# Moving the stationary weight blocks of a decoder trunk 224 bytes aside in SBUF

## The chip, the cores and the metric

The kernel runs on one core of a Trainium2 chip. The metric is the device time of one execution in microseconds. The kernel before takes 851.81 us, the median of three runs (850.81 to 852.27 us).

## The reference, cut to what matters

A two-layer decoder trunk over 256 tokens with 1024 features, all in float32. Layer 0 mixes tokens with a gated unit (gMLP), layer 1 with an mLSTM; behind each stand a LayerNorm with residual, a SwiGLU feed-forward, a second LayerNorm and a gated embedding.

```
for i in range(DEPTH):                       # DEPTH = 2
    y = gmlp_mixer(x, ...) if i % 2 == 0 else mlstm_mixer(x, ...)
    x = layer_norm(ALPHA * x + y, ln1_g[i], ln1_b[i])
    x = layer_norm(ALPHA * x + (silu(x @ w_gate) * (x @ w_up)) @ w_down, ln2_g[i], ln2_b[i])
    x = x + sigmoid(x @ ple_w_gate[i] + ple_b_gate[i]) * (p[i] @ ple_w_proj[i])
```

Nearly all of the arithmetic is the products with the weights: `gm_w_in`, `gm_w_out`, `ml_w_in`, `ml_w_out`, `ffn_w_gate`, `ffn_w_up`, `ffn_w_down` and `ple_w_gate`.

## The kernel before, in words

Every product is done with float32 numbers split in two float32r parts, hi and lo: `a @ b` becomes hi·hi + lo·hi + hi·lo, three matmuls into one PSUM bank. The weights come from HBM in blocks of 128 partitions by 1024 float32 (512 KB). For each block SyncE loads a `raw` tile, ScalarE casts it to the hi half of a tile `w`, and VectorE subtracts to get the lo half (`split`, L134 to L136). `weight_plan` writes down the order of all blocks; `weight` (L175) hands out the next one and keeps loads eight blocks and casts four blocks ahead of their use. A `w` tile has 2 × 1024 float32, 8192 bytes in each partition, and the pool keeps six such slots; blocks that are used for longer lie in the wider pool `b8`.

There are two ways in which a block meets x or a hidden state.

- As the moving operand (`mm_tok`, L206 to L209, and `mm_part`): 128 tokens of the other operand are the stationary 128 columns, and 512 columns of the weight stream past them. So run the gMLP's v columns (`vps`), all down projections (`acc`), the first 512 columns of gate, up and z (`first`, `zf`), and the embedding's gate (`gate`).
- As the stationary operand (`mm_feat`, L211 to L214, called by `feat_from_x`, L216): 128 columns of the weight are loaded, and x^T, 256 tokens in `xh` (hi) or `xl` (lo), streams past. A block gives 8 × 3 = 24 such matmuls. So run the gMLP's u columns (`ups`, 24 blocks), the mLSTM's xm columns (`xmps`, 16), the later z columns (`zps`, 12), and the later gate and up columns of both layers (`pg` and `pu`, 36 each).

Each MATMUL on TensorE has its own LDWEIGHTS, which loads the stationary 128 columns of that matmul while the matmul before it still streams; the profile shows these loads as an engine of their own, PEld.

In SBUF the program lays every large tile at a multiple of 512 bytes. `xh` and `xl` hold 8 pieces of 1024 bytes, a `w` tile 2 × 8 pieces of 512 bytes. So a stationary piece of `w` and the x^T piece that streams meanwhile both start at a multiple of 512.

The order of work is written out by hand in the loops; no scheduler changes it. TensorE's order around the change is, for a step of the gMLP: 24 matmuls of `ups`, 4 of `svps`, 12 of `acc`; for a step of the feed-forward: 24 of `pg`, 24 of `pu`, 12 of `acc`; for a step of the mLSTM: 24 of `xmps`, then a dozen small ones for q, v, the gates and the scores, and at some steps 24 of `zps`. The gates' matmuls (`psG`, L691 and L700) are a case of their own: x^T's place is taken by `xm`, 256 columns as well, and the stationary operand `wx` has only 16 columns.

Of the kernel before, what the change touches and what calls it, by code (L numbers as in the profile page):

```python
# [9 lines left out]
F32R = mybir.dt.float32r  # L10
# [4 lines left out]
P = 128  # L15
D = 1024
# [30 lines left out]
WIDE = {(n, l, k) for l in range(2) for n, m in (("g", 4), ("u", 2), ("pg", 6)) for k in range(m)}  # L47
# [5 lines left out]
def down_blocks(f):  # L53

    return range(4) if f == 3 + LAG else [f - LAG] if f > 3 + LAG else []


def weight_plan(a):
# [17 lines left out]
    def ffn(l):  # L76
        add(("pj", l, 0), a["ple_proj"][l, 0])
        for n in ("g", "u"):
            for kp in range(4):
                add((n, l, kp), a["ffn_" + n][l, kp])  # L80
        for f in range(4, NF + LAG):
            for n in ("g", "u") if f < NF else ():
                add((n, l, f), a["ffn_" + n][l, f])
            for e in down_blocks(f):
                add(("d", l, e), a["ffn_d"][l, e])
        add(("pj", l, 1), a["ple_proj"][l, 1])
        for k in range(KD):
            add(("pg", l, k), a["ple_gate"][l, k])
# [28 lines left out]
def trunk(ctx, tc, a, out):  # L117
# [10 lines left out]
    def tl(tag, shape, dt=F32, name="t"):  # L128
        return sb.tile(shape, dt, tag=tag, name=name, bufs=BUFS[tag])
# [4 lines left out]
    def split(hi, lo, src, fast=False, sub=dve):  # L134

        return dve.tensor_copy(hi, src) if fast else act.copy(hi, src), sub.tensor_tensor(lo, src, hi.bitcast(F32), ALU.subtract)  # L136
# [7 lines left out]
    def issue_after(ops):  # L144

        stack = ExitStack()
        for op in ops:
            stack.enter_context(tc.issue_after(op.ins))
        return stack
# [3 lines left out]
    def ahead(loads, casts):  # L153
        while at["load"] < min(len(plan), at["use"] + loads):
            ap = plan[at["load"]][1]
            n = ap.shape[-1]
            t = tl("raw", [P, n], name="raw")
            for c in HALF if at["load"] == 0 else [slice(0, n)]:
                sp.dma_start(t[:, c], ap[:, c])
            raws[at["load"]] = t  # L160
            at["load"] += 1
        while at["cast"] < min(len(plan), at["use"] + casts):
            i = at["cast"]
            key, raw = plan[i][0], raws.pop(i)
            n = raw.shape[-1]
            t = tl("b8" if key in WIDE else "w", [P, 2, D], F32R, "w")
            with issue_after(behind["cast"]):
                for c in HALF if i == 0 else [slice(0, n)]:
                    split(t[:, 0, c], t[:, 1, c], raw[:, c], fast=i == 0 and c.start == 0)
            wt[i] = t  # L170
            at["cast"] += 1
# [3 lines left out]
    def weight(*key, casts=None):  # L175
        at["use"] = max(at["use"], place[key])
        ahead(LOAD_AHEAD, CAST_AHEAD if casts is None else casts)
        at["use"] = max(at["use"], place[key] + 1)
        return wt.pop(place[key])
# [126 lines left out]
    for i in range(4):  # L306
        t = tl("m2", [P, 2, S], name="xr")
        if i == 0:
            for k in range(2):
                act.dma_start(t[:, k, :], a["xT"][i, :, k, :])  # L310
        else:
            sp.dma_start(t, a["xT"][i])
        ahead(1 + i, int(i == 0))
        xr.append(t)
    make_identity(nc, ident)
    pool.memset(mhalf, -0.5)
    for i in range(4):
        for k in ((0,), (1,)) if i == 0 else ((0, 1),):
            c, cr = slice(2 * i + k[0], 2 * i + k[-1] + 1), slice(k[0], k[-1] + 1)
            split(xh[:, c, :], xl[:, c, :], xr[i][:, cr, :], fast=c.start == 0)  # L320
            ahead(LOAD_AHEAD, 1 + i)

    vs = []
    for c in range(6):
# [21 lines left out]
        for kp in range(4):  # L346
            w = weight("v", c, kp)
# [90 lines left out]
    def channel_mixer(l, acc, last, hook=None):  # L438
# [60 lines left out]
        for f in range(4, NF + LAG):  # L499
            if f < NF:  # L500
                gate_up(f)
            if f == 4:
                transpose_h(1)
                acc = Down(NF)
            for e in down_blocks(f):
                acc.add(e, hs.pop(e), weight("d", l, e, casts=1 if f >= NF else None))
            if f == 14 and hook:
                hook()
            if f == NF - 1:
                ahead(LOAD_AHEAD, LAG + 1)  # L510
# [449 lines left out]
```

## Time and profile before

| | |
|---|---|
| median of three runs | 851.81 us |
| the profiled execution, its own time | 852.55 us |
| its span, first to last instruction | 850.8 us |
| TensorE busy (matmuls) | 842.0 us, 99% of the span |
| weight loads on TensorE busy | 761.8 us, 90% |
| VectorE, ScalarE, GpSimd busy | 580.2, 452.9, 154.9 us |
| DMA queue of the loads | 54.3% of 16 engines' time |
| mean granted TensorE clock | 0.999 |

A matmul's time in the profile runs from its start to a modelled end behind the array's drain, and the next one starts before that end. So how fast matmuls follow each other is read from start to start, not from the duration of one.

### The profile page before, as it was taken

To read this page: it belongs to the slowest core of one execution; us is meant where nothing else is said; L and a number is where in the kernel's file an instruction comes from. 1 tells how busy PE (TensorE), PEld (TensorE's weight loads), DVE (VectorE), ACT (ScalarE), POOL (GpSimd) and SP (SyncE) were. 2 spreads that over 40 slices of the span, in tenths; PEclk is the share of its full clock that TensorE was granted. 3 is DMA by queue.
4 is the path that set the end of the run, shared out by engine and by line. 5 is a ranking of instruction groups with operands and counts; after the bars stand their busy time and mean duration, and the time that the engine had idled before them with its cause. 6 is when DMAs were issued, how large, how long until landed. Compare 5 with 4: busy or idle time off the path is not lost.

```text
span 850.8 us, 13770 instructions
## 1 busy us (share of the span) xinstructions
PE 842.0 (99%) x5367; PEld 761.8 (90%) x5367; DVE 580.2 (68%) x831; ACT 452.9 (53%) x722; POOL 154.9 (18%) x197
## 2 busy tenths in 40 slices
PE   8999999999999999999999999999999999999997
PEld 6889999998889999999879999998888999999986
DVE  6667985676955555465868877688895555466574
ACT  6556655455444444365247767777643444455422
POOL 1021653443100001500102333233310000000010
PEclk9999999999999999999999999999999999999999
DMA  8885465567375555577234444263745655577601
GB/s 296 294 290 175 149 201 176 173 204 262 119 266 183 194 179 189 177 256 261 70 122 148 153 127 136 74 235 108 240 161 197 207 178 195 176 244 251 197 2 50
DMA packets 44714, 155.62 MB, mean 183 GB/s; under 512 B 5224, under 2 KB 5992, under 8 KB 44648
## 3 DMA queue, kind: packets, MB, share of 16 engines
q1 hardware_dynamic: 44360, 154.47, 54.3%
q8 instruction: 42, 0.69, 0.3%
q10 hardware_dynamic: 288, 0.26, 0.1%
q14 instruction: 24, 0.20, 0.1%
HBM read 153.67 MB, written 1.05 MB: 182 GB/s over the span
## 4 chain that ended last, share of the span: by engine, by line
PE 95%; DVE 2%; DMA 1%; POOL 0%; ACT 0%; issue 0%; DVEq 0%; SPq 0%; ACTq 0%
PE acc L207 9%; PE acc L208 9%; PE acc L209 9%; PE pu L214 4%; PE pu L213 4%; PE pu L212 4%; PE pg L214 4%; PE pg L213 4%; PE pg L212 4%; PE ups L214 3%; PE ups L213 3%; PE vps L207 3%; PE ups L212 3%; PE vps L208 3%; PE vps L209 3%; PE xmps L212 2%
## 5 line engine op out<-in xcount | busy, mean ns | idle before, releaser
L136 DVE TENSOR_TENSOR w<-raw,w 128x1024 fp32r<-128x1024 f32 (+1 forms) x277 | 334.5, 1219 | 168.0 <-ACT w L136 167.2
L136 ACT CAST w<-raw 128x1024 fp32r<-128x1024 f32 (+1 forms) x276 | 284.7, 1040 | 200.2 <-issue 54.5
L207 PE MATMUL acc<-w,h 128*128 128x512 f32 x336 | 131.8, 392 | 0.9 <-ACT hn L833 0.9
L208 PE MATMUL acc<-w,h 128*128 128x512 f32 x336 | 131.5, 391 | 0.2 <-DVE h L136 0.2
L209 PE MATMUL acc<-w,h 128*128 128x512 f32 x336 | 130.7, 389 | 0.0
L212 PE MATMUL pg<-xh,w 128*128 128x256 f32 x288 | 81.6, 283 | 0.0
L214 PE MATMUL pu<-xh,w 128*128 128x256 f32 x288 | 81.5, 283 | 0.0
L212 PE MATMUL pu<-xh,w 128*128 128x256 f32 x288 | 81.5, 283 | 0.0
L213 PE MATMUL pu<-xl,w 128*128 128x256 f32 x288 | 81.5, 283 | 0.0
L214 PE MATMUL pg<-xh,w 128*128 128x256 f32 x288 | 81.5, 283 | 0.0
L213 PE MATMUL pg<-xl,w 128*128 128x256 f32 x288 | 81.5, 283 | 0.0
L209 PEld LDWEIGHTS acc<-w,h 128*128 128x128 f32 x336 | 63.1, 188 | 13.5
L207 PEld LDWEIGHTS acc<-w,h 128*128 128x128 f32 x336 | 63.3, 188 | 13.0 <-ACT hn L833 1.3
L208 PEld LDWEIGHTS acc<-w,h 128*128 128x128 f32 x336 | 63.3, 188 | 11.5 <-DVE h L136 0.6
L212 PEld LDWEIGHTS pg<-xh,w 128*128 128x128 f32 x288 | 55.1, 191 | 1.3
L213 PEld LDWEIGHTS pg<-xl,w 128*128 128x128 f32 x288 | 55.1, 191 | 1.3
L265 POOL TENSOR_SCALAR ve<-mv 128x1 f32<-128x1 f32 x8 | 6.2, 776 | 273.8 <-DVE mv L285 273.8
L212 PEld LDWEIGHTS pu<-xh,w 128*128 128x128 f32 x288 | 55.3, 192 | 0.0
L213 PEld LDWEIGHTS pu<-xl,w 128*128 128x128 f32 x288 | 55.3, 192 | 0.0
L214 PEld LDWEIGHTS pu<-xh,w 128*128 128x128 f32 x288 | 55.3, 192 | 0.0
L214 PEld LDWEIGHTS pg<-xh,w 128*128 128x128 f32 x288 | 55.1, 191 | 0.0
L214 PE MATMUL ups<-xh,w 128*128 128x256 f32 x192 | 54.3, 283 | 0.0
(237 smaller groups left out, 1806.9 us busy)
## 6 DMA issues: line engine op xcount, KB each, us to landing
raw<-in_ffn_g SPq DMA_DIRECT2D x44, 512.0 KB, 3.5
raw<-in_ffn_u SPq DMA_DIRECT2D x44, 512.0 KB, 3.5
raw<-in_ffn_d SPq DMA_DIRECT2D x44, 512.0 KB, 3.6
raw<-in_gm_u SPq DMA_DIRECT2D x24, 512.0 KB, 3.5
raw<-in_gm_wo SPq DMA_DIRECT2D x24, 512.0 KB, 3.5
raw<-in_gm_v SPq DMA_DIRECT2D x23, 512.0 KB, 4.9
raw<-in_ple_gate SPq DMA_DIRECT2D x16, 512.0 KB, 4.4
raw<-in_ml_z SPq DMA_DIRECT2D x16, 512.0 KB, 3.5
```

The costliest lines, as they stand in the source:

```text
L136: return dve.tensor_copy(hi, src) if fast else act.copy(hi, src), sub.tensor_tensor(lo, src, hi.bitcast(F32), ALU.subtract)
L207: pe.matmul(ps, lh, w[:, 0, c], start=start, stop=False)
L208: pe.matmul(ps, ll, w[:, 0, c], start=False, stop=False)
L209: pe.matmul(ps, lh, w[:, 1, c], start=False, stop=stop)
L212: pe.matmul(ps, w[:, 0, c], h, start=start, stop=False)
L213: pe.matmul(ps, w[:, 0, c], l, start=False, stop=False)
L214: pe.matmul(ps, w[:, 1, c], h, start=False, stop=stop)
L265: pool.tensor_scalar(ve[:, :n], var, EPS, None, ALU.add)
```

## The change

The slot of a `w` tile grows by 128 float32, from 8192 to 8704 bytes in each partition. A block that will be stationary is placed 56 float32 (224 bytes) behind the slot's start; any other block of that pool stays at the start. `stationary` names the blocks: u of the gMLP, xm, z from the fifth on, and gate and up of the feed-forward from the fifth on, 124 blocks in all. `b8` tiles, `xh`, `xl` and the hidden states keep their sizes. All slots still begin at a multiple of 512 bytes, since 8704 is 17 × 512. No instruction is added, removed or moved on any engine; what changes are the addresses that ScalarE and VectorE write and TensorE loads from.

```
+ASIDE = 56
+
+def stationary(key):
+    return key[0] in ("u", "xm") and len(key) == 2 or key[0] in ("g", "u", "z") and key[-1] >= 4
...
-            t = tl("b8" if key in WIDE else "w", [P, 2, D], F32R, "w")
+            if key in WIDE:
+                t = tl("b8", [P, 2, D], F32R, "w")
+            else:
+                first = ASIDE if stationary(key) else 0
+                t = tl("w", [P, 2 * D + P], F32R, "w")[:, first:first + 2 * D]
+                t = t.rearrange("p (i n) -> p i n", i=2)
```

## Rows read from the trace of the kernel before

**Rows 1.** The page: busy time by engine, then the chain that ended last.
```profile
PE 842.0 (99%) x5367; PEld 761.8 (90%) x5367; DVE 580.2 (68%) x831; ACT 452.9 (53%) x722; POOL 154.9 (18%) x197
PE 95%; DVE 2%; DMA 1%; POOL 0%; ACT 0%; issue 0%; DVEq 0%; SPq 0%; ACTq 0%
```

**Rows 2.** Waits of TensorE: total us, times, longest us.
```profile
PE vps L207 <- DVE w L136: 1.2, 1, 1.2
...
PE acc L208 <- DVE h L136: 0.2, 1, 0.2
```

**Rows 3.** TensorE's groups by line: shapes, count | busy us, mean ns | idle before.
```profile
L207 PE MATMUL acc<-w,h 128*128 128x512 f32 x336 | 131.8, 392 | 0.9 <-ACT hn L833 0.9
...
L213 PE MATMUL pu<-xl,w 128*128 128x256 f32 x288 | 81.5, 283 | 0.0
...
L213 PE MATMUL pg<-xl,w 128*128 128x256 f32 x288 | 81.5, 283 | 0.0
...
L213 PE MATMUL ups<-xl,w 128*128 128x256 f32 x192 | 54.3, 283 | 0.0
...
L213 PE MATMUL xmps<-xl,w 128*128 128x256 f32 x128 | 36.2, 283 | 0.0
...
L213 PE MATMUL zps<-xl,w 128*128 128x256 f32 x96 | 27.1, 283 | 0.0
...
L273 PE MATMUL tp<-ident,xn 128*128 128x128 f32 x80 | 10.6, 273 | 0.0
```

**Rows 4.** Timeline of TensorE, end of a u block: start us, duration us.
```profile
199.98 0.28 PE L212 MATMUL ups<-xh,w 128*128 128x256 f32 x1
...
202.38 0.28 PE L214 MATMUL ups<-xh,w 128*128 128x256 f32 x1
202.50 0.64 PE L393 MATMUL svps<-ws,vn 128*128 128x256 f32 x4
```

**Rows 5.** Timeline of the weight loads over the same stretch.
```profile
199.98 0.19 PEld L213 LDWEIGHTS ups<-xl,w 128*128 128x128 f32 x1
200.10 0.19 PEld L214 LDWEIGHTS ups<-xh,w 128*128 128x128 f32 x1
```

**Rows 6.** Timeline of TensorE, twelve acc matmuls behind a u block.
```profile
123.68 0.40 PE L207 MATMUL acc<-w,h 128*128 128x512 f32 x1
...
124.84 0.39 PE L209 MATMUL acc<-w,h 128*128 128x512 f32 x1
...
126.42 0.28 PE L212 MATMUL ups<-xh,w 128*128 128x256 f32 x1
```

**Rows 7.** Timeline of TensorE in the mLSTM: the gates' matmuls and their neighbours.
```profile
478.27 0.40 PE L691 MATMUL gates<-xm,wx 128*16 128x256 f32 x2
478.50 0.28 PE L212 MATMUL qps<-xm,bdm 128*128 128x256 f32 x1
```

**Rows 8.** Weight loads by line: of x^T matmuls, transposes, gates.
```profile
L212 PEld LDWEIGHTS pu<-xh,w 128*128 128x128 f32 x288 | 55.3, 192 | 0.0
...
L273 PEld LDWEIGHTS tp<-ident,xn 128*128 128x128 f32 x80 | 9.4, 140 | 1.5
...
L691 PEld LDWEIGHTS gates<-xm,wx 128*16 128x16 f32 x32 | 3.1, 96 | 0.3
```

**Rows 9.** Timeline of TensorE: eight transposes in a row.
```profile
605.86 1.04 PE L842 MATMUL tp<-ident,hn 128*128 128x128 f32 x8
```

**Rows 10.** Casts of the weight blocks by line: shapes, count | busy us, mean ns | idle before.
```profile
L136 DVE TENSOR_TENSOR w<-raw,w 128x1024 fp32r<-128x1024 f32 (+1 forms) x277 | 334.5, 1219 | 168.0 <-ACT w L136 167.2
L136 ACT CAST w<-raw 128x1024 fp32r<-128x1024 f32 (+1 forms) x276 | 284.7, 1040 | 200.2 <-issue 54.5
```

**Rows 11.** Stretches: window us, then busy of PE, PEld, DVE, ACT, POOL, clock, DMA share, GB/s.
```profile
0.00:20.00 20.00, 17.52 (x61) 12.44 (x62) 12.06 (x20) 12.12 (x15) 2.53 (x14) 1.00 0.86 305
...
250.00:440.00 190.00, 189.10 (x1243) 173.51 (x1243) 114.39 (x146) 87.34 (x123) 19.06 (x33) 1.00 0.55 184
...
470.00:560.00 90.00, 90.00 (x734) 86.47 (x733) 71.11 (x132) 66.11 (x147) 27.63 (x30) 1.00 0.41 137
```

## Prediction

> **What bounds the kernel now.** I read the page's shares first: TensorE is busy 99% of the span and holds 95% of the chain that ended last [rows 1]. The list of what TensorE waits for has five rows, the longest wait 1.2 us and the shortest 0.2 us [rows 2]. So the whole span is a row of matmuls, and a change can move the time in two ways only: by the distance from one matmul's start to the next one's, or by making TensorE wait for what it does not wait for now.
>
> The distance has to come from the timeline, since the group list gives 283 ns for a matmul of 256 columns whatever follows it. In the tail of a u block the starts run from 199.98 to 202.50 us over 21 matmuls [rows 4]: 2.52 / 21 = 0.120 us. The weight load for the next matmul starts in the same hundredth of a microsecond as the matmul that streams (199.98 in both rows) and the loads too are 0.12 us apart [rows 4, 5]. The two run side by side for nearly the whole distance: 128 stationary columns from `w`, 256 moving columns from `xh` or `xl`.
>
> Is 120 ns what the array needs for 256 columns? Two rows say that it is more. Eight transposes in a row take 1.04 us from the first start to the last end [rows 9]; with 0.273 us for the last one (the same kind at L273) [rows 3] that is (1.04 - 0.273) / 7 = 0.110 us from start to start, at a load of 128 columns each. The two gates' matmuls stream 256 columns as an x^T matmul does, but their stationary operand has 16 columns, a load of 96 ns in place of 192, both with the load's latency in them [rows 8]; they take 478.50 - 478.27 = 0.23 us [rows 7], 0.115 each. So 5 to 10 ns of the 120 are not the moving columns' own.
>
> Third, matmuls of one form do not always keep one distance. Of twelve `acc` matmuls behind a u block the first five starts take 124.84 - 123.68 = 1.16 us, 0.232 each, and the other seven 126.42 - 124.84 = 1.58 us, 0.226 each [rows 6]. Shape, tiles' kinds and load are the same; what differs is what ran before, that is, how far the load and the moving stream are apart in time. A load and a stream that disturb each other would look like this, and an offset in the address is another way of setting them apart. I take that as the mechanism; the trace shows that it is a few ns a matmul, not that the address sets it.
>
> The Trainium skill says otherwise: "TensorE: Matmul & The Clock Gate", in the step on LDWEIGHTS, has two independent SBUF read ports, one for the moving operand and one for the loads, so that loading the next weights takes nothing from the running matmul. [...] By the ports alone an address could do nothing, and the sum below would be zero; that is the first rival. The 0.232 against 0.226 speaks against the ports being all of it.
>
> **The change part by part.** Nothing is issued, waited for or moved that was not before; the addresses change.
>
> First, the x^T matmuls. The five groups have 288, 288, 192, 128 and 96 rows at L213 [rows 3], 992 together, and as many at L212 and at L214: 2976 matmuls, at 120 ns 357 us of the span. What one of them takes when its stationary piece starts 224 bytes off is not in the trace. The bounds come from the nearest rows:
> - least: 110 ns, the transposes. 10 × 2976 = 29.8 us gained.
> - nearest: 115 ns, the gates, where 256 columns of float32r stream and hardly a load stands beside them. 5 × 2976 = 14.9 us gained.
> - most: the disturbed `acc` matmuls are 232 - 226 = 6 ns over the undisturbed ones. If the offset puts the load where it disturbs more than now, 6 × 2976 = 17.9 us lost.
> I take 115: it is the same stream with the neighbour taken nearly away, and the 120 of now is the distance of two reads that start in the same hundredth of a microsecond at the same place of a 512-byte row, so that a shift has more room below than above.
>
> Second, the `acc` matmuls behind them. If the lag that the x^T block leaves behind goes, the first five lose 1.16 - 5 × 0.226 = 0.03 us in each group; about 22 groups in the gMLP and 18 in each feed-forward, 58, are 1.7 us. They could as well gain a lag. I count nothing, with 1.7 us to either side.
>
> Third, the casts. ScalarE's 1040 ns and VectorE's 1219 ns a block [rows 10] now write 224 bytes further on; I know no row in which such a write stands at another offset. Were they 10% longer, VectorE would have some 0.12 us more a block. In the feed-forward VectorE is busy 114.39 of 190 us, ScalarE 87.34 [rows 11], and TensorE's waits are next to nothing, so casts stand four blocks ahead and the cover is 75 us. Counted at nothing. Without the cover it would be 124 blocks × 0.12 = 15 us.
>
> Fourth, what a quicker TensorE asks of the others. In the feed-forward a step has 48 x^T matmuls, 0.24 us less of some 8.5 (60 matmuls, 48 × 0.120 + 12 × 0.227); the loads go from 184 GB/s to about 190, against 305 moved in the first 20 us [rows 11]. VectorE goes from 60 to 62%. The narrowest place is the mLSTM's middle: VectorE 71.11 and ScalarE 66.11 of 90 us [rows 11], 79 and 73%. There some of the gain can turn into waits. xm and z have (128 + 96) × 3 = 672 matmuls, 3.4 us of the 14.9; I take off a fourth of it, 0.9 us.
>
> Fifth, the longer slots take 3 KB more in each partition and shift the tiles behind them by a multiple of 512; no instruction waits for that.
>
> Sum against the profiled execution's own 852.55 us, 1.75 over its span: 852.55 - 14.9 + 0.9 = 838.6. The median of the runs is 0.74 less than the profiled one, so 837.8 us; I say 838.
>
> **The rivals.**
>
> *Nothing happens.* The two reads don't meet, or they meet whatever the offset, because the stream runs through a piece faster than the load and comes past it once anyway. The 120 ns are then a cost of changing weights in the array. For it: every x^T piece shows the same 0.120 and the same 283 ns [rows 3, 4], though pieces lie at even and odd multiples of 512; the gates' 16-column loads start at any multiple of 64 and still need 0.115, most of the excess over 0.110. Against it: 0.232 and 0.226 in one row of equal matmuls [rows 6]. Time: 852, give or take the 0.2%, about what a measurement of this kernel can tell from no change, 1.7 us.
>
> *Slower, by a load that meets the stream in its middle.* Now load and stream start together and part at once, the stream being faster. With the load 224 bytes ahead in the row, the stream catches up with it half-way, and every x^T matmul pays what the first `acc` matmuls pay. Half of the worst price, 3 ns, gives 3 × 2976 = 8.9 us, 861 us; the full 6 ns give 870. It decides from 0.6 ns a matmul on, since 0.6 × 2976 = 1.8 us is the 0.2%. For it: a lag between the two does cost in `acc`. Against it: the same lag on the way from `acc` into x^T has no row with a longer distance.
>
> *All of the excess goes.* The x^T matmuls come down to the transposes' 110 ns, and the lag in `acc` goes too: 851.8 - 29.8 - 1.7 + 1.7 (a fourth of the mLSTM's 672 × 10 ns, as above) = 822 us. For it: the transposes reach that distance beside loads of 128 columns. Against it: their loads are of another kind, 140 ns against 192 [rows 8], and the gates keep 115 with hardly a load.
>
> **How the numbers follow.** Faster to between 110 and 119 ns, with 115 the likeliest: 0.50. All of the excess gone: 0.09. Nothing, within 0.2%: 0.22. Slower: 0.19. So faster 0.59, same 0.22, slower 0.19. The forecast is 838 us; its own range is 826 to 848. For 8 in 10 the range must take in the case of no change as well: from 822, the floor by the transposes, to 854; what is left out is most of the slower case.
>
> **What will show it.** Starts in a u block 0.115 us apart: about 2.42 us over 21 matmuls where they are now 2.52. The x^T matmuls and their loads become a few ns shorter than 283 and 192 if the disturbance is inside them. The `acc` distances in the steady part, the transposes and the gates stay as they are. TensorE's list of waits stays under 6 us, any new one in the mLSTM and on VectorE's casts. A distance of 0.120 with 283 ns shows the first rival; over 0.121 the second. The forecast would be wrong too if starts come closer and the span does not shrink: then waits must have grown by as much.

## The result and the profile after

The changed kernel takes 844.22 us (median of four runs, 843.4 to 845.14) against 851.65 us for the kernel before on the same chips: a ratio of 0.9915, 95% interval 0.9902 to 0.9927. The forecast was 838 us, in a range of 822 to 854. The span of the profiled execution fell from 850.8 to 843.4 us.

The page's shares and TensorE's waits of the kernel after, with the matmuls' lines now numbered 15 higher and the casts' 9, answer to [rows 1, 2]:

```profile
PE 834.7 (99%) x5367; PEld 753.3 (89%) x5367; DVE 580.1 (69%) x831; ACT 452.4 (54%) x722; POOL 156.1 (19%) x197
...
PE 90%; DVE 5%; DMA 2%; ACT 1%; POOL 1%; issue 1%; DVEq 0%; POOLq 0%; ACTq 0%; SPq 0%
```
```profile
PE warm L319 <- DVE warm L316: 1.2, 1, 1.2
PE acc L222 <- ACT hn L848: 0.8, 1, 0.8
PE vps L222 <- DVE w L145: 0.7, 1, 0.7
...
PE num L824 <- POOL plo L145: 0.2, 1, 0.2
```

TensorE is as busy as before and waits no more than before, six waits of 4.1 us in all where there were five of 4.4; the gain came from matmuls that follow each other more closely. The same 21 distances at the end of a u block as in [rows 4], and the weight loads beside them:

```profile
198.73 0.28 PE L227 MATMUL ups<-xh,w 128*128 128x256 f32 x1
...
201.18 0.40 PE L408 MATMUL svps<-ws,vn 128*128 128x256 f32 x2
```
```profile
199.55 0.19 PEld L229 LDWEIGHTS ups<-xh,w 128*128 128x128 f32 x1
199.67 0.19 PEld L227 LDWEIGHTS ups<-xh,w 128*128 128x128 f32 x1
199.79 0.19 PEld L228 LDWEIGHTS ups<-xl,w 128*128 128x128 f32 x1
```

(201.18 - 198.73) / 21 is 0.1167 us, where [rows 4] gave 0.1200. Not every block does so well: 16 of the 28 in the mLSTM hold 117.8 ns at the same 224 bytes, those that come behind the small `s` matmuls and those behind such a block. One of them, over the same 21 distances, (473.24 - 470.77) / 21 = 0.1176:

```profile
470.77 0.28 PE L227 MATMUL xmps<-xh,w 128*128 128x256 f32 x1
...
473.24 0.65 PE L704 MATMUL vps<-w,xm 128*128 128x256 f32 x4
```

The groups by line show the gain inside the instructions too, matmuls of 279 to 280 ns for 283 [rows 3] and loads of 188 for 192 [rows 8], while a transpose stays at 272 (273 before):

```profile
L228 PE MATMUL pg<-xl,w 128*128 128x256 f32 x288 | 80.5, 280 | 0.0
L228 PE MATMUL pu<-xl,w 128*128 128x256 f32 x288 | 80.4, 279 | 0.0
...
L288 PE MATMUL tp<-ident,xn 128*128 128x128 f32 x80 | 10.5, 272 | 0.0
```
```profile
L227 PEld LDWEIGHTS pu<-xh,w 128*128 128x128 f32 x288 | 54.1, 188 | 0.0
```

The twelve `acc` matmuls behind a u block, which answer to [rows 6], have not changed inside: five of 1.16 / 5 = 0.232, then 0.227 each.

```profile
195.63 0.40 PE L222 MATMUL acc<-w,h 128*128 128x512 f32 x1
...
196.79 0.39 PE L224 MATMUL acc<-w,h 128*128 128x512 f32 x1
...
198.15 0.40 PE L224 MATMUL acc<-w,h 128*128 128x512 f32 x1
198.38 0.28 PE L227 MATMUL ups<-xh,w 128*128 128x256 f32 x1
```

Summed over both traces, start to start: the distances from one x^T matmul to the next shrank by 8.4 us, those from x^T into `acc` by 0.2; those from `acc` into x^T grew by 0.4 (the last `acc` of a group now streams beside a load that lies aside, 235 ns for 226), and those within `acc` by 0.4. The start and the rest of the matmuls took another 0.4 us more, net of changes in both directions. The span's 7.4 us are accounted for.

### The profile page after: what moved, and what is told of

Read it like the earlier page. It is cut to its first block, busy times and chain, and to the rows that moved or that the text cites. A ratio compares the mean times of both kernels' runs of the same rounds, so it can differ in the third digit from the quotient of the medians.

```text
span 843.4 us, 13770 instructions
## 1 busy us (share of the span) xinstructions
PE 834.7 (99%) x5367; PEld 753.3 (89%) x5367; DVE 580.1 (69%) x831; ACT 452.4 (54%) x722; POOL 156.1 (19%) x197
## 4 chain that ended last, share of the span: by engine, by line
PE 90%; DVE 5%; DMA 2%; ACT 1%; POOL 1%; issue 1%; DVEq 0%; POOLq 0%; ACTq 0%; SPq 0%
PE acc L222 9%; PE acc L223 9%; PE acc L224 9%; PE pg L228 4%; PE pg L227 4%; PE pu L227 4%; PE pu L228 4%; PE pg L229 4%; PE pu L229 4%; PE vps L222 3%; PE vps L224 3%; PE vps L223 3%; PE ups L228 2%; PE ups L227 2%; PE ups L229 2%; PE xmps L227 2%
## 5 line engine op out<-in xcount | busy, mean ns | idle before, releaser
L145 DVE TENSOR_TENSOR w<-raw,w 128x1024 fp32r<-128x1024 f32 (+1 forms) x277 | 333.7, 1217 | 166.7 <-ACT w L145 166.0
L145 ACT CAST w<-raw 128x1024 fp32r<-128x1024 f32 (+1 forms) x276 | 284.6, 1041 | 200.9 <-issue 48.4
L227 PE MATMUL pg<-xh,w 128*128 128x256 f32 x288 | 80.7, 280 | 0.0
L229 PE MATMUL pg<-xh,w 128*128 128x256 f32 x288 | 80.4, 279 | 0.0
L227 PE MATMUL pu<-xh,w 128*128 128x256 f32 x288 | 80.4, 279 | 0.0
L229 PE MATMUL pu<-xh,w 128*128 128x256 f32 x288 | 80.3, 279 | 0.0
L227 PEld LDWEIGHTS pg<-xh,w 128*128 128x128 f32 x288 | 54.1, 188 | 1.3
L229 PEld LDWEIGHTS pg<-xh,w 128*128 128x128 f32 x288 | 54.1, 188 | 0.0
L227 PEld LDWEIGHTS pu<-xh,w 128*128 128x128 f32 x288 | 54.1, 188 | 0.0
L229 PEld LDWEIGHTS pu<-xh,w 128*128 128x128 f32 x288 | 54.1, 188 | 0.0
L228 PE MATMUL ups<-xl,w 128*128 128x256 f32 x192 | 53.7, 280 | 0.0
```

The source lines that it names most:

```text
L227: pe.matmul(ps, w[:, 0, c], h, start=start, stop=False)
L228: pe.matmul(ps, w[:, 0, c], l, start=False, stop=False)
L229: pe.matmul(ps, w[:, 1, c], h, start=False, stop=stop)
```

## The experiments

**Where the load lies, block by block.** Theory A: the distance hangs on how far the load's place is ahead of the moving stream's. Theory B: only the alignment of the load counts. The first run gave each block an offset of its own.

```
...
-first = ASIDE if stationary(key) else 0
+first = aside(key)      # 0 to 127 float32, by block
```


> Every stationary weight block gets an offset of its own, from 0 to 508 bytes (gMLP u blocks 0 to 15 in steps of 32 bytes, the next eight at odd multiples of 16, layer 0 gate in steps of 4 bytes, layer 0 up in steps of 28). Theory A (what counts is how far the load's place is ahead of the stream's): the mean distance of x^T matmuls is a curve over the offset with 120.0 ns at 0 and 116.7 ns at 224 bytes; 224 need not be its lowest point, and neighbours 32 bytes apart differ by little; the curve repeats wherever an offset is used again. Theory B (only whether the load starts at a multiple of 512, or of some smaller power of two, counts): two or three levels, 120.0 for aligned offsets and 116.7 for all others. Total between 840 and 852 us either way.

847.44 us, against 851.55 for the kernel before beside it. The mean distance in the steady part of a block, the 18 distances from its sixth start to its 24th: 120.0 ns at 0 bytes, 118.4 at 16, 122.4 at 24, 116.7 at 28, 117.8 at 64, 120.0 at 160, 117.8 at 192, 116.4 at 224 (116.7 over twelve distances, after which its row repeats), and again 120.0 at 256, 117.8 at 320, 120.0 at 416, 117.8 at 448, 116.4 at 480. So 0 and 256 are alike, as 64, 192 and 224 are to 320, 448 and 480; but 24 and 280 are not (122.4 and 118.7). Many levels, none a matter of being aligned or not: theory B falls. What I had not expected: neighbours 4 bytes apart differ by up to 5.7 ns (24 and 28), single blocks stood at 113.3 (168, 308 and 436 bytes, and 64, 320 and 448 in the mLSTM), and 224 itself stood at 117.8 in many mLSTM blocks. The blocks at 256, 24 and 28 bytes in turn, 0.120, (305.43 - 302.87) / 21 = 0.122 and (313.70 - 311.25) / 21 = 0.117:

```profile
107.92 0.28 PE L243 MATMUL ups<-xh,w 128*128 128x256 f32 x1
...
110.44 0.64 PE L424 MATMUL svps<-ws,vn 128*128 128x256 f32 x4
```
```profile
302.87 0.28 PE L243 MATMUL pg<-xh,w 128*128 128x256 f32 x1
...
305.43 0.28 PE L243 MATMUL pu<-xh,w 128*128 128x256 f32 x1
```
```profile
311.25 0.28 PE L243 MATMUL pg<-xh,w 128*128 128x256 f32 x1
...
313.70 0.28 PE L243 MATMUL pu<-xh,w 128*128 128x256 f32 x1
```

**Moving x^T too, or x^T alone.**

```
+xh, xl = (sb.tile([P, KD * S + P], F32R, name=n)[:, XOFF:XOFF + KD * S]... for n in ("xh", "xl"))
 # first run: XOFF = 56, ASIDE = 56      second run: XOFF = 72, ASIDE = 0
```


> x^T hi and lo lie 224 bytes behind a multiple of 512 as well, so load and stream start at the same place again. Theory A: x^T matmuls back to 120.0 ns, the total near 852 us but for what the products do whose stationary operand is x^T and whose moving operand stays at the multiple. Theory B (place of the load alone): 116.7 ns stays, 844 us.

854.65 us. With both 224 bytes aside the u block is back at (118.39 - 115.87) / 21 = 0.1200:

```profile
115.87 0.28 PE L229 MATMUL ups<-xh,w 128*128 128x256 f32 x1
...
118.39 0.28 PE L410 MATMUL svps<-ws,vn 128*128 128x256 f32 x1
```

It is 3.1 us slower than the kernel before (one run each) since the matmuls of 512 columns whose stationary operand is x^T and whose moving weights stay at the multiple went from 226.7 to 233.3 ns: the v columns, the first columns of gate, up and z, and the embedding's gate. For the v columns, (61.38 - 59.98) / 6 = 0.233:

```profile
59.98 0.39 PE L224 MATMUL vps<-w,xh 128*128 128x512 f32 x1
...
61.38 0.39 PE L224 MATMUL vps<-w,xh 128*128 128x512 f32 x1
```

> The weight blocks lie at the multiple of 512 as in the kernel before, x^T lies 288 bytes behind one, so that the load is 224 bytes ahead of the stream modulo 512 with no load off its multiple. Theory A, with a period of 512: 116.7 ns and about 844 us. Theory B: 120.0 ns and about 852 us.

847.34 us. No weight block lies aside here, x^T alone does, and the u block keeps the distance of the change, (118.04 - 115.59) / 21 = 0.1167; the total is above the change's since here too those matmuls of 512 columns stand at 233.3 ns:

```profile
115.59 0.28 PE L229 MATMUL ups<-xh,w 128*128 128x256 f32 x1
...
118.04 0.28 PE L410 MATMUL svps<-ws,vn 128*128 128x256 f32 x1
```

So at this offset it is the difference of the two places that counts, and not where either lies: theory A, shown from both sides.

**The blocks that are the moving operand.**

```
+    if key[0] == "wo":
+        return 8 * key[1] if key[1] < 16 else 8 * (key[1] - 16) + 4
...                 # d, v and mo likewise; stationary blocks stay at 56
```


> On top of the change, the blocks that are a moving operand (gMLP v and output, down projections, mLSTM output) get offsets from 0 to 508 bytes while their stationary operands stay at multiples of 512. Theory A: the distances of these 512-column matmuls move too, by up to 3 or 4 ns around 226.7. Theory B: 226.7 stays at every offset. A third theory, that a load hinders the stream only where the load ends close to the stream's end (256 columns, not 512), also gives 226.7. Total 840 to 850 us.

849.62 us, 5 us over the change. Here the multiples of 256 are among the good places: 226.7 ns at 0 and 256 in steady rows, and as good at 28, 252 and 364; 228 to 237 at every other offset. Two `acc` groups of the feed-forward, at 0 and at 416 bytes; the last seven distances are (262.24 - 260.65) / 7 = 0.227 and (354.59 - 352.95) / 7 = 0.234:

```profile
260.65 0.39 PE L240 MATMUL acc<-w,h 128*128 128x512 f32 x1
...
262.24 0.40 PE L238 MATMUL acc<-w,h 128*128 128x512 f32 x1
```
```profile
352.95 0.40 PE L240 MATMUL acc<-w,h 128*128 128x512 f32 x1
...
354.59 0.28 PE L243 MATMUL pg<-xh,w 128*128 128x256 f32 x1
```

Theory A again, with a larger price than its 3 to 4 ns; theory B and the third theory, which gave 226.7 everywhere, fall. The place that is poor for 256 moving columns is among the best for 512.

**Is it the reading?** Everything back at multiples of 512; the load, the stream or both of the x^T products read one column over and over.

```
+h, l = (t[:, 0:1].to_broadcast([P, S]) for t in (h, l))                          # layers 0, 1: stream
...
+wk = [w[:, i, k * P:k * P + 1].to_broadcast([P, P]) for i in range(2)]           # gMLP, layer 0: load
```


> On the kernel before (everything at multiples of 512), with part of the computation replaced: the x^T products read one column over and over, so the results of those products are not the reference's. In the gMLP the load reads one weight column 128 times, in layer 1's feed-forward the stream reads one x^T column 256 times, in layer 0's feed-forward both do. Theory A (reads of load and stream hinder each other in SBUF, by their addresses): 120 ns falls to about 110 where both stay in one place, and changes in the other two. Theory C (120 is what changing weights costs in the array, and the addresses act in some other way): 120 ns stays in all three.

835.85 us. One column for both, layer 0: (256.55 - 254.21) / 21 = 0.111. One column for the stream alone, layer 1: (705.78 - 703.43) / 21 = 0.112. One column for the load alone, gMLP: (116.56 - 114.11) / 21 = 0.1167. In steady rows the first two are one and the same, 111.7 ns.

```profile
254.21 0.28 PE L227 MATMUL pu<-xh,w 128*128 128x256 f32 x1
...
256.55 0.40 PE L207 MATMUL acc<-w,h 128*128 128x512 f32 x1
```
```profile
703.43 0.28 PE L227 MATMUL pu<-xh,w 128*128 128x256 f32 x1
...
705.78 0.40 PE L207 MATMUL acc<-w,h 128*128 128x512 f32 x1
```
```profile
114.11 0.28 PE L227 MATMUL ups<-xh,w 128*128 128x256 f32 x1
...
116.56 0.40 PE L403 MATMUL svps<-ws,vn 128*128 128x256 f32 x2
```

The same instructions, the same columns and the same changes of weights take 8 ns less when the stream stays in one place. Theory C, that 120 is what changing weights costs in the array, falls: at most 112 can be that, and the other 8 ns come of reading. How much of the 8 is the two reads meeting, this run alone does not say, for a stream of one column might be quicker by itself; but an offset of the load with every column read takes 6.7 of them away (436 bytes, below). The Trainium skill, "TensorE: Matmul & The Clock Gate", in the step on LDWEIGHTS, has a load take nothing from the running matmul's SBUF reading; the runs differ from it: with the load's reading alone changed, 120.0 became 116.7 here, and with the load's place alone changed, 116.7 in the change. The measurement decides.

**Does the offset alone set the distance?** The three offsets of 113.3 ns and 64, each for a whole stage, then at other stages.

```
 # first run:  ups 168, layer 0 308, layer 1 436, xm and z 64 bytes
 # second run: ups 308, layer 0 168, layer 1 64, xm and z 436 bytes
```


> One offset for all stationary blocks of a stage: 168 bytes in the gMLP, 308 in layer 0's feed-forward, 436 in layer 1's, 64 in the mLSTM. In the sweep single blocks stood at 113.3 ns at 168, 308 and 436, and 64 gave 113.3 in the mLSTM but 117.8 elsewhere. Theory A1 (the offset alone sets the distance): 113.3 ns in all of gMLP and both feed-forwards, some 838 us in all. Theory A2 (the offset allows several distances, and what ran before picks one): 113.3 in part of the blocks only, 116 to 120 in others, 842 to 847 us.

844.92 us, against 851.66 before. Theory A2: at 168 bytes, two u blocks of one run stand at (88.94 - 86.56) / 21 = 0.113 and (104.49 - 101.97) / 21 = 0.120. The block around 86.56 us comes behind four `svps` matmuls, the one around 101.97 behind a group of `acc`. At 168 bytes in the gMLP and at 308 in layer 0 all blocks behind `acc` hold 0.120; at 436 in layer 1 all of those hold 0.113. The matmuls just before are not the whole of it: the block at 82.86 us stands behind `svps` too and holds 0.120.

```profile
86.56 0.28 PE L238 MATMUL ups<-xh,w 128*128 128x256 f32 x1
...
88.94 0.28 PE L419 MATMUL svps<-ws,vn 128*128 128x256 f32 x1
...
101.97 0.28 PE L238 MATMUL ups<-xh,w 128*128 128x256 f32 x1
...
104.49 0.28 PE L419 MATMUL svps<-ws,vn 128*128 128x256 f32 x1
```

> The same offsets at other stages: 308 bytes in the gMLP, 168 in layer 0's feed-forward, 64 in layer 1's, 436 in the mLSTM. Theory A1: 113.3 ns for 308, 168 and 436 wherever they stand, and one value for 64. Theory A2: the values of an offset differ from those of the run beside it, since other matmuls come before.

846.35 us. 168 and 308 settle at 120.0 behind `acc` in either stage; 64 is 117.8 behind `acc` and 113.3 in most of the mLSTM; 436 is 113.3 at both stages where it stood, but for six blocks that hold 118, three near the start of a stage and three late in the mLSTM. So the place allows a few distances, and one of them is taken by what ran before, as far as the runs show: blocks of one offset behind groups of `acc` repeat the same distance, one after the other. A1 falls. Of A2's words for this run, that an offset's values would differ from the run beside it, 64 bytes is the plain case; 168 and 308 behind `acc` kept theirs.

**One better offset for all, and a finer sweep behind `acc`.**

```
-ASIDE = 56
+ASIDE = 109        # 436 bytes
```


> All stationary blocks 436 bytes aside in place of 224. In the runs before this one 436 held 113.3 ns in nearly all blocks of layer 1 and of the mLSTM. Theory A (place of the load against the stream, with the matmuls before picking among a few distances): 113.3 to 114 ns wherever the block comes behind acc, 2976 x 6.5 ns = 19 us under the kernel before, less some 0.5 us of longer last acc starts: 832 to 835 us, ratio 0.977 to 0.981. If gMLP and layer 0 pick another distance (as 308 and 168 did), 838 to 845 us.

836.83 us, ratio 0.9833 (0.9814 to 0.9852). A u block: (121.84 - 119.46) / 21 = 0.113; one of the 15 that hold 0.118, none of them behind `acc`, is the second fence, from the start of the gMLP:

```profile
119.46 0.28 PE L227 MATMUL ups<-xh,w 128*128 128x256 f32 x1
...
121.84 0.40 PE L408 MATMUL svps<-ws,vn 128*128 128x256 f32 x2
```
```profile
82.70 0.28 PE L227 MATMUL ups<-xh,w 128*128 128x256 f32 x1
...
85.18 0.29 PE L408 MATMUL svps<-ws,vn 128*128 128x256 f32 x1
```

Theory A's mechanism, with a time that misses its 832 to 835 by 1.8 us: 15.9 us off the x^T distances, not 19.

> One offset for gate and up of a step, so that a block is seen both behind acc and in its own row: 4 to 72 bytes in layer 0, 76 to 144 in layer 1, 148 to 240 in the gMLP, all in steps of 4 bytes; 436 in the mLSTM from its fifth xm block on. Theory A: distances between 112 and 123 ns in a few levels, with no rule by multiples of 16 or 32 bytes, and the same for gate and up of a step where the distance does not hang on what ran before. Theory B (alignment of the load alone): two levels.

847.25 us. Gate and up of a step agree within 0.5 ns at 35 of 36 offsets (at 24 bytes they differ by 1.3), over many levels from 113.3 to 123.3 ns, where a few were expected. 113.3 came at 88 and 180 bytes behind `acc`, and at 76, whose gate block came behind transposes, not `acc`. 180 is 436 less 256. Of the 64 offsets from 4 to 256 bytes, 37 stand more than 1 ns below 120, 25 within 1 ns of it and 2 more than 1 ns above. The best and the worst u block, 180 and 204 bytes, (110.10 - 107.72) / 21 = 0.113 and (146.60 - 144.01) / 21 = 0.123:

```profile
107.72 0.28 PE L240 MATMUL ups<-xh,w 128*128 128x256 f32 x1
...
110.10 0.28 PE L421 MATMUL svps<-ws,vn 128*128 128x256 f32 x1
```
```profile
144.01 0.29 PE L240 MATMUL ups<-xh,w 128*128 128x256 f32 x1
...
146.60 0.65 PE L421 MATMUL svps<-ws,vn 128*128 128x256 f32 x4
```

**The other two offsets that held 113.3.** `ASIDE = 22` (88 bytes) and `ASIDE = 19` (76 bytes), in place of 56.

> All stationary blocks 88 bytes aside. In the fine sweep 88 held 113.3 ns behind acc and in its own row. Theory A: as 436 bytes, 113.3 ns in nearly all steady rows, 833 to 838 us, ratio near 0.983. If single blocks of a sweep don't stand for a whole run (as 308 and 168 did not), 118 to 120 ns and 846 to 852 us.

835.99 us, ratio 0.982 (0.9803 to 0.9836), the best median of the study. Nearly all steady rows are at 113.3 (10 of 124 blocks hold 116.7 or 120); a block's first distances are longer, so that a u block's 21 come to (127.83 - 125.44) / 21 = 0.114:

```profile
125.44 0.28 PE L227 MATMUL ups<-xh,w 128*128 128x256 f32 x1
...
127.83 0.40 PE L408 MATMUL svps<-ws,vn 128*128 128x256 f32 x2
```

> All stationary blocks 76 bytes aside. As for 88: 113.3 ns and 833 to 838 us by theory A, ratio near 0.983; 846 to 852 us if the sweep's single blocks don't stand for a whole run. Blocks behind a wait may hold 118 as at 436.

836.78 us, ratio 0.9833 (0.9818 to 0.9848). Three blocks hold 120, two of them the first gate and up block of layer 0, and all behind `acc` hold 113.3. So 88 did for a whole run what its block behind `acc` did in the sweep; 76 did as well, though the sweep had not seen it there. The three offsets of 113.3 cannot be told apart by their intervals; each beats the change's 224 bytes, whose interval begins at 0.9902.

## Why the prediction was right

The bound: right. TensorE stayed at 99% of the span (90% of the chain that ended last, for 95%), and the change acted through the distance of starts alone.

The mechanism, taken from the `acc` rows [rows 6]: right that the reads of load and stream cost a few ns by where they lie, and shown by the runs, from both operands' side and by taking the reads away. The first rival, that nothing happens, fell with the result. But that 224 bytes would be quicker, and not the same or slower, no row of before could tell. In the fine sweep 37 of 64 offsets are quicker by over 1 ns, with 224 among the nine best, so the sign is in part luck; the prediction's 0.59 for faster was a fair chance.

The size: the one term that was off is the distance of an x^T matmul. It was taken as 115 from the gates' row [rows 7] and measured 116.7 in steady rows. That would still be 3.3 × 2976 = 9.8 us; the 2976 distances gave 8.6, since 16 mLSTM blocks hold 117.8 and the first distance of a block did not shrink. The gates were the nearest row by shape but no measure of what an offset does: with the stream kept in one column the distance is 112, and the offset has levels from 113.3 to 123.3, and 224 bytes is among the better ones but not at the lowest. Nothing in the trace before could have told which.

The lower bound came of a wrong reading. The transposes' 110 ns was set against 256 columns of float32r, but a transpose moves 128 columns of plain float32 [rows 9], so that it says nothing of what an x^T matmul needs. That 110 is close to the 111.7 of a stream that reads one column is luck.

The slower rival exists, with about its price, at other offsets: at 204 bytes an x^T matmul takes 3.3 ns more than at the multiple, and moving blocks lose 2 to 10 ns nearly wherever they lie aside. Its picture, a stream that catches up with the load half-way, was not tested.

The casts, counted at nothing: VectorE 1217 ns a block and ScalarE 1041, for 1219 and 1040 [rows 10]. The 0.9 us for waits in the mLSTM was not needed: TensorE's longest wait is still 1.2 us, and the one new wait, in the mLSTM, is 0.2. The lag in `acc`, counted at nothing with 1.7 to either side, cost 0.4, and the step back into x^T another 0.4.

What stays open: which addresses within 256 bytes disturb each other, and why the distance locks at 113.3 for 76, 88, 180 and 436 and at 120 for 168 and 308 once `acc` ran before. The runs show that it does, not the rule. That it is what ran before, and not something else of the moment, which picks the distance is inferred from blocks that repeat; no run changed that alone.

## What to carry to other kernels

Where TensorE is busy all the time, divide a row of starts by its count and compare it with a row of the same columns and type whose loads or streams are different: a constant excess of some per cent may be the load and the stream disturbing each other, and moving one operand's start by a few bytes changes it at no cost in instructions, here for 3 KB more of each partition. Choose the offset by a sweep inside one run, one offset a block, read behind the matmuls that really come before; then try the best ones for the whole kernel. Sweep both uses apart: here multiples of 256 were among the best for 512 moving columns and poor for 256.

## What the runs showed of the hardware

- A float32r matmul of 256 columns beside a load of 128 columns: 120.0 ns from start to start when both operands start at the same place modulo 256 (the kernel before, and 256 bytes; the run with both at 224), 113.3 to 123.3 at the 64 offsets of the fine sweep, 111.7 when the stream reads one column only.
- For 512 columns: 226.7 ns at the same place and at 28, 252 and 364 bytes, 228 to 237 at all other offsets tried.
- An estimate from the two, if a column costs the same in both forms: 2 × 120.0 - 226.7 = 13.3 ns of a matmul at the same place do not grow with its columns. That leaves 106.7 for 256 columns, so that at the best offsets, 113.3, the fixed part is 6.6, half of it.
- Start addresses 4 bytes apart can differ by 6.7 ns a matmul (204 and 208 bytes: 123.3 and 116.6); the same address can hold 113.3 or 120.0 in different blocks of one run (168 bytes). Most blocks keep one distance for their 24 matmuls; with 308 bytes in the gMLP three settled on 113.3 only after some ten distances of 114 to 120.
- ScalarE's and VectorE's casts ran equally long into a tile 224 bytes aside: 1041 and 1217 ns over all blocks, for 1040 and 1219; over the 124 blocks that moved, 1048 and 1226, for 1046 and 1232.
